# Row buffers opened ahead of retrieval, gathers paced to 31/32 of the dense steps, one inverse root on VectorE, the look-up in two pieces

## The chip, the cores and the metric

The kernel runs on one core of a Trainium2 chip. The metric is the device time of one execution in microseconds (us). TensorE, VectorE, ScalarE, POOL (GpSimd) and SyncE (which issues most of the DMAs) each work through their own instructions in order and wait for one another by semaphores. TensorE's clock has two levels, 1.2 and 2.4 GHz; the profile gives the granted clock as a share of the higher one.

## What is computed

One decoder block on 1024 tokens of width 1024, in float32: a gated DeltaNet and a sliding-window attention side by side, then an expert layer, a gated embedding, and a last norm. The change touches the expert layer and what follows it:

```
x = x + concat(o_dn, o_sw) @ w_out
h = rmsnorm(x, ffn_norm)
q = (h @ wq) per head and half;  sc = q @ keys          # 8 heads, 2 halves, 128 keys
top 16 of each half -> 256 sums -> top 16 of these       # expert = i1 * 128 + i2, gates = softmax
x = x + sum over 8 x 16 experts: gate * gelu(h . u[e]) * v[e]     # 16384 experts of width 1024
x = x + sigmoid(rmsnorm(x, ple_norm) @ w_gate) * (p @ w_proj)
out = rmsnorm(x, final_norm)
```

## The kernel before, in words

Tokens are worked on in 8 blocks of 128. `upstream` (L327) does the projections (`project`), the mixers (`mixing`: `deltanet` and `swa`) and, in four groups of two blocks, `retrieve` (L398): output projection, norm, queries, scores, top 16 of each half (`first_topk`), then `topk` (L757). Matmul operands are split into a high and a low float32r part, and three products are added up (`mm3`, L141).

The expert layer is done in two ways at once. Blocks 0 to 4 (`DBLK`) are dense: `topk` turns their choices into one-hot tiles, `gbuild` (L837) builds a table `gd` of gates for every expert and token, and `dense` (L924) goes over all 16384 experts in 128 tiles. Four tiles make a group (`cg`, 32 groups): for each tile `uT` and `v` are loaded and split, 48 matmuls form `bk_u`, ScalarE takes the gelu, VectorE multiplies by `Gt` and splits the result into `wh` and `wl`; then for 5 blocks and 2 halves 12 matmuls each form `bk_y`, which VectorE adds to `xB`. The banks of the first two blocks are held over all groups.

Blocks 5 to 7 (`ABLK`) are gathered: for each of 128 choices `fetched` (L856) has POOL issue an indirect DMA of one row for each of 128 tokens, from `u` and later from `v`. VectorE takes a dot product with `h2n` for each `u` row (L868) and adds each `v` row to `acc` with the weight from `dots` (L882). `h2n` and `acc` share one buffer. The 768 gathers are one generator (`gather_job`), and `dense` calls `step` (L946) 448 times, after each expert tile and each `bk_y`; a call advances the gathers to their share of the steps done. `held_back` puts each gathered row's VectorE work behind the dense work of `LAG` steps earlier.

Row buffers come in turns from two pools: even rows from `gp` (`GBUF`), odd ones from `gx` (`GXBUF`). `gp` also holds `h2n`/`acc` and `dots`. Both are opened after `upstream` (L1069, L1070), on the right side of SBUF, which is filled from its end: the pools of `retrieving` (L383; `lt` with `tv`, `tiu`, `sc`, `cand`, `get3` first, then `wp2`, `hp`, `sm2`, `bg`) have lain there before, and then come `xB` and the `v` tiles. A tile laid over an older one waits for that one's last reader.

The look-up in `topk` (L784 to L808) finds the two indices behind each of the 16 best sums by comparisons against starts, with tiles of 16 x KC x 8; KC = 16 is all in one piece.

`final` (L1013) takes the blocks in the order 5, 6, 0, 1, 2, 3, 4, 7: `pre` (L1033) loads a block, takes its norm (`norm`, L187: ScalarE's square sum, `rsqrt`, one VectorE step `h`) and transposes it; `post` (L1047) multiplies by the gate weights. These are loaded in 8 slices through two `raw` buffers and split into `wgh` and `wgl` (`gate_weights`, L1020). `rsqrt` (L154) is two POOL instructions: scale and add, then the power -0.5.

The order of instructions on each engine and in each DMA queue is not written by hand: a planner lays it out at build time from the program's order, the waits, and its own estimate of times. At run time each engine keeps to it.

Of the kernel before, what the change touches and what calls it, by code (L numbers as in the profile page):

```python
# [7 lines left out]
F32 = mybir.dt.float32  # L8
F32R = mybir.dt.float32r
BF = mybir.dt.bfloat16  # L10
I32 = mybir.dt.int32
U32 = mybir.dt.uint32
AF = mybir.ActivationFunctionType
ALU = mybir.AluOpType
# [4 lines left out]
P = 128  # L19
# [5 lines left out]
EPS = 1e-6  # L25
# [8 lines left out]
NU = len(DBLK) * 128  # L34
GC = 4
TB = 16
GBUF = 4
GXBUF = 3
RATE = 0.6
LAG = 2  # L40
HELD = 2
# [26 lines left out]
def block_kernel(ctx: ExitStack, tc, I, out, dbg=None):  # L68
# [9 lines left out]
    def tt(o, a, b, op):  # L78
        return V.tensor_tensor(o, a, b, op)  # L79

    def stt(o, a, s, b, op0, op1, **k):
        return V.scalar_tensor_tensor(o, a, s, b, op0, op1, **k)  # L82
# [65 lines left out]
    h2Td = [dr.tile([P, DK, NU], F32, name=f"h2Td{i}") for i in range(2)]  # L148
    gd = dr.tile([NE // GC, P, NT // TB, GC, TB], F32, name="gd")

    eidx = cp.tile([P, len(UBLK), P], I32, name="eidx")
    gate_a = cp.tile([P, len(UBLK), P], F32, name="gate_a")

    def rsqrt(pool, dst, src, scale, n):  # L154
        v = pool.tile([P, n], F32, tag=f"rsv{n}", name="rs_v", bufs=2)
        G.tensor_scalar(v, src, scale, EPS, op0=ALU.mult, op1=ALU.add)  # L156
        G.tensor_tensor(dst, v, mhalf[:, 0:n], ALU.pow)  # L157
# [169 lines left out]
    def upstream():  # L327
        with early as em:
            dn = em.enter_context(tc.tile_pool(name="dn", bufs=1, reuse_waits="tile"))
            psum(em, dn=2, de=1, sw=1)  # L330
            with ExitStack() as es:
                c1 = es.enter_context(tc.tile_pool(name="c1", bufs=1, side="right"))
                wp = es.enter_context(tc.tile_pool(name="wp", bufs=3, side="right"))
                sm = es.enter_context(tc.tile_pool(name="sm", bufs=2, side="right"))
                psum(es, acc=2, tp=2)
                projected(wp, sm)
                load_consts()
                mixw = row(c1, "mix_norm", D)
                convw = c1.tile([P, 12, 4], F32, name="convw")
                nc.sync.dma_start(convw, I["convw"])  # L340
                onorm = row(c1, "out_norm", P)
                V.tensor_scalar(onorm, onorm, 0.5, None, op0=ALU.mult)
                dtb = row(c1, "dt_bias", 4)
                nea = row(c1, "a_log", 4)
                S.activation(nea, nea, AF.Exp)
                V.tensor_scalar(nea, nea, -1.0, None, op0=ALU.mult)
                prevs = c1.tile([P, 12, 3], F32, name="prevs")
                halo[:] = [(mixw, convw, onorm, dtb, nea), prevs]
                rope_tables(sm, cos, sin)
                project(0, (c1, wp, sm))  # L350
                mixers = mixing(dn)
                mixers(0)
                project(1, (c1, wp, sm))
            with ExitStack() as es:
                lt = es.enter_context(tc.tile_pool(name="lt", bufs=1, side="right", reuse_waits="tile"))
                retrieve, half_built = retrieving(lt, es)
                for gi in range(len(GROUPS)):
                    if gi + 1 < len(GROUPS):
                        mixers(gi + 1)
                    elif HBLK:  # L360
                        half_built()
                    retrieve(gi)
# [394 lines left out]
    def topk(tk, bg, b, v, iu):  # L757
# [25 lines left out]
        tt(dx[:, 1:16], ix[:, 0, 1:16], ix[:, 0, 0:15], ALU.subtract)  # L783
        flat = cand.rearrange("p h c -> p (h c)")  # L784
        i1, i2 = flat[:, 0:P], flat[:, P:2 * P]
        KC = 16

        def summed(dst, x):
            for s in (1, 2, 4):
# [134 lines left out]
    def dense(xB):  # L924
        with ExitStack() as es:
# [20 lines left out]
            def step(ins):  # L946
                anchors.append(ins.ins)
                count[0] += 1
                n = total * count[0] // steps - count[1]
                count[1] += n  # L950
                advance(n)

# [60 lines left out]
    def final(xB):  # L1013
        with ExitStack() as es:
            fq = es.enter_context(tc.tile_pool(name="fq", bufs=1, reuse_waits="tile"))
            fp = es.enter_context(tc.tile_pool(name="fp", bufs=2, reuse_waits="tile"))
            cf = es.enter_context(tc.tile_pool(name="fc", bufs=1, reuse_waits="tile"))
            psum(es, g=4, tp=4)

            def gate_weights():  # L1020
                for k in range(DK):
                    hi = cf.tile([P, D], F32R, name=f"wgh{k}")
                    lo = cf.tile([P, D], F32R, name=f"wgl{k}")
                    raw = cf.tile([P, D], F32, tag="raw", name="raw", bufs=2)
                    nc.sync.dma_start(raw, I["wg"][k])
                    split(raw, hi, lo)
                    wg.append((hi, lo))

            wg = []
            plew = row(fp, "ple_norm", D, 1)  # L1030
            order = ABLK[:-1] + BBLK + ABLK[-1:]

            def pre(b):  # L1033
                if b in ABLK:
                    xt = fp.tile([P, D], F32, tag="xt", name="xt", bufs=3)
                    nc.sync.dma_start(xt, x1d[b])
                else:
                    xt = xB[:, b - BBLK[0]]
                pr = fq.tile([P, D], F32, tag="pr", name="pr", bufs=3)
                nc.sync.dma_start(pr, prd[b])  # L1040
                h = norm(fp, "h", xt, plew, 2)
                hh = fp.tile([P, DK, P], F32R, tag="hh", name="hh")
                hl = fp.tile([P, DK, P], F32R, tag="hl", name="hl")
                transpose_split("tp", h, hh, hl, slice(0, P))
                return b, xt, pr, hh, hl

            def post(b, xt, pr, hh, hl):  # L1047
                for j in range(2):
                    cs = slice(j * 512, (j + 1) * 512)
                    pg = bank("g")  # L1050
                    for dk in range(DK):
                        mm3(pg, hh[:, dk], hl[:, dk], wg[dk][0][:, cs], wg[dk][1][:, cs],
                            dk == 0, dk == DK - 1)
                    gt = fq.tile([P, 512], F32, tag="gt", name="gt", bufs=2)
                    S.activation(gt, pg, AF.Tanh, scale=0.5)
                    stt(gt, gt, 1.0, pr[:, cs], ALU.add, ALU.mult)
                    tt(xt[:, cs], gt, xt[:, cs], ALU.add)
                o = norm(fq, "o", xt, finw, 2)
                nc.sync.dma_start(out[b * P:(b + 1) * P, :], o)

            nxt = pre(order[0])
            gate_weights()
            finw = row(fq, "final_norm", D, 1)
            for i in range(NBLK):
                cur, nxt = nxt, pre(order[i + 1]) if i + 1 < NBLK else None
                post(*cur)

    upstream()
    pools["gp"] = ctx.enter_context(tc.tile_pool(name="gp", bufs=GBUF, side="right", reuse_waits="tile"))  # L1069
    pools["gx"] = ctx.enter_context(tc.tile_pool(name="gx", bufs=GXBUF, side="right", reuse_waits="tile"))  # L1070
    with tc.tile_pool(name="xB", bufs=1, side="right", reuse_waits="tile") as xp:
        xB = xp.tile([P, NB, D], F32, name="xB")
# [61 lines left out]
```

## Time and profile before

| | us |
|---|---|
| median of 3 runs | 3034.56 |
| lowest, highest | 3032.35, 3036.15 |
| the profiled execution | 3043.6 |
| its span, first to last instruction | 3041.8 |
| mean granted clock of TensorE | 0.986 |

The profile is one execution. Its page gives the busy time of each engine; views of the trace behind it show single instructions with their start, their length and, in brackets, how long the engine had been idle and what ended that idle time. PE is TensorE's matmuls, PEld its weight loads, DVE VectorE, ACT ScalarE, SP SyncE (SPq: the DMAs that it issues). L12 is line 12 of the kernel. Matmuls are pipelined, so their lengths overlap. Windows are counted from the start of the span.

### The profile page before, as it was taken

The page shows a single profiled execution, that of the slowest core. Times are in us where ns is not written, and L with a number is a line of the kernel's source. Part 1 is how long each engine was busy: PE and PEld are TensorE (multiplying, and loading weights), DVE is VectorE, ACT ScalarE, POOL GpSimd, SP SyncE. Part 2 cuts the span into 40 slices and gives each one's busy share as a digit, 9 for nine tenths or more (in the row PEclk, how much of TensorE's full clock was granted, in tenths as well). Part 3 has the DMA queues.
Part 4 walks back from the last instruction along what each step waited for, and adds up shares of the span by engine and source line. Part 5 has one row for each costly group of instructions (what it writes and reads, how often), then busy time and mean ns, then how long its engine had stood idle before and what let it go on. Part 6 is the DMA issues. An engine that isn't in the chain of part 4 may idle for free. (4 is left out here: it accounts for less than half of the span.)

```text
span 3041.8 us, 49726 instructions
## 1 busy us (share of the span) xinstructions
PE 2936.2 (97%) x18287; PEld 2690.0 (88%) x18287; DVE 2499.4 (82%) x5023; ACT 1234.6 (41%) x2761; POOL 1068.4 (35%) x901
## 2 busy tenths in 40 slices
PE   7999999999999889999999999999999999999988
PEld 5887999999998789999999989998898898998967
DVE  5658636898999779988699889887998898899974
ACT  5556634488777663222222222232232232222223
POOL 0000000000000000765356556554656565556541
PEclk9989999999999999999999999999999999999989
DMA  7569657689889994999799989888999899899962
GB/s 236 142 223 364 206 191 248 215 223 243 237 242 270 287 279 141 351 338 348 272 342 354 330 319 369 329 332 300 335 351 345 318 358 332 306 337 347 324 256 89
DMA packets 449955, 869.30 MB, mean 286 GB/s; under 512 B 193456, under 2 KB 235824, under 8 KB 445360
## 3 DMA queue, kind: packets, MB, share of 16 engines
q1 hardware_dynamic: 339120, 463.43, 46.5%
q0 software_dynamic: 110592, 402.70, 36.4%
q8 instruction: 143, 2.34, 0.3%
q14 instruction: 100, 0.82, 0.1%
HBM read 766.40 MB, written 99.61 MB: 285 GB/s over the span
## 5 line engine op out<-in xcount | busy, mean ns | idle before, releaser
L136 PE MATMUL bk_u<-hT,uh 128*128 128x320 f32 x4096 | 915.4, 310 | 7.0 <-DMA hT<-h2Td 3.7
L136 PEld LDWEIGHTS bk_u<-hT,uh 128*128 128x128 f32 x4096 | 695.7, 189 | 23.2 <-ACT ge L988 4.6
L858 POOL DMA_INDIRECT rows<-in_u_dram,eidx x384 | 499.1, 1300 | 555.5 <-DVE dots L868 283.1
L136 PE MATMUL bk_u<-hT,ul 128*128 128x320 f32 x2048 | 635.0, 310 | 0.3 <-DVE ul L79 0.3
L858 POOL DMA_INDIRECT rows<-in_v_dram,eidx x384 | 498.6, 1298 | 350.1 <-DVE acc L82 287.5
L82 DVE SCALAR_TENSOR_TENSOR acc<-rows,dots,acc 128x1024 f32<-128x1024 f32 x384 | 492.2, 1282 | 35.4 <-DMA rows<-in_v_dram,eidx 24.5
L868 DVE CUSTOM_DVE_ANT_0 rows<-rows,h2n 128x1024 f32<-128x1024 f32 x384 | 459.9, 1223 | 27.5 <-DMA rows<-in_u_dram,eidx 27.3
L136 PEld LDWEIGHTS bk_u<-hT,ul 128*128 128x128 f32 x2048 | 386.5, 189 | 4.1 <-DVE ul L79 0.7
L988 ACT ACTIVATE ge<-bk_u 128x320 f32<-128x320 f32 x256 | 109.8, 431 | 603.3 <-PE bk_u L136 552.6
L136 PE MATMUL bk_y<-vh,wh 128*128 128x512 f32 x768 | 298.9, 391 | 3.0 <-DVE xB L79 3.0
L136 PE MATMUL bk_y<-vl,wh 128*128 128x512 f32 x768 | 299.9, 392 | 0.0
L136 PE MATMUL bk_y<-vh,wl 128*128 128x512 f32 x768 | 296.8, 393 | 2.6 <-DVE wl L79 2.6
L76 ACT ACTIVATE wh<-ge 128x320 fp32r<-128x320 f32 x256 | 118.7, 469 | 316.7 <-DVE ge L79 304.1
L76 ACT ACTIVATE o<-o,tT 128x128 f32<-128x128 f32 x640 | 204.5, 392 | 56.4 <-DVE o L79 55.1
L76 ACT ACTIVATE uh<-ur 128x1024 fp32r<-128x1024 f32 x128 | 135.3, 1057 | 226.4 <-PE bk_u L136 217.5
L136 PE MATMUL bk_gm<-o 128*128 128x128 f32 x1280 | 203.2, 286 | 22.5 <-ACT o L76 16.2
L136 PE MATMUL bk_s<-h,whi 128*128 128x256 f32 x1024 | 209.1, 295 | 3.3 <-DMA whi<-wqc 1.0
L79 DVE TENSOR_TENSOR o<-iota,tT 128x1024 f32<-128x1024 f32 x160 | 194.7, 1220 | 11.5 <-PE bk_gm L136 8.9
L136 PEld LDWEIGHTS bk_gm<-o 128*128 128x128 f32 x1280 | 178.2, 195 | 29.0 <-ACT o L76 20.2
L136 PE MATMUL bk_yp<-vl,wh 128*128 128x512 f32 x512 | 199.7, 391 | 0.0
L136 PE MATMUL bk_yp<-vh,wh 128*128 128x512 f32 x512 | 199.1, 391 | 0.0
L79 DVE TENSOR_TENSOR xB<-bk_y,xB 128x512 f32<-128x512 f32 x192 | 131.1, 689 | 79.5 <-PE bk_y L136 79.1
(302 smaller groups left out, 5840.5 us busy)
## 6 DMA issues: line engine op xcount, KB each, us to landing
ur<-in_uT_dram SPq DMA_DIRECT2D x128, 512.0 KB, 6.8
vr<-in_v_dram SPq DMA_DIRECT2D x128, 512.0 KB, 6.7
gd<-stage SPq DMA_DIRECT2D x40, 1024.0 KB, 7.3
Gt<-gd SPq DMA_DIRECT2D x32, 1280.0 KB, 9.6
wlo<-wqc SPq DMA_DIRECT2D x128, 256.0 KB, 4.6
whi<-wqc SPq DMA_DIRECT2D x128, 256.0 KB, 4.7
whi<-woc SPq DMA_DIRECT2D x64, 256.0 KB, 4.8
wlo<-woc SPq DMA_DIRECT2D x64, 256.0 KB, 4.7
```

The source lines that it names most:

```text
L76: return S.activation(o, i, AF.Copy, **k)
L79: return V.tensor_tensor(o, a, b, op)
L82: return V.scalar_tensor_tensor(o, a, s, b, op0, op1, **k)
L136: PE.matmul(o, l, r, start=start, stop=stop)
L858: G.indirect_dma_start(out=r, out_offset=None, in_=tab, in_offset=bass.IndirectOffsetOnAxis(ap=eidx[:, u, s:s + 1], axis=0))
L868: held_back(V.tensor_tensor_reduce(out=r, in0=r, in1=h2n, op0=ALU.mult, op1=ALU.add, scale=1.0, scalar=0.0, accum_out=dots[:, s:s + 1]))
L988: S.activation(ge, pa, AF.Gelu_apprx_tanh)
```

## The change

`gp` is opened within `upstream`, ahead of the retrieval pools, with three row buffers instead of four; `gx`, still opened afterwards, gets four instead of three. The look-up runs twice on halves. `step` divides by 31/32 of the steps. The first `pre` of `final` uses an inverse root on VectorE: an integer first guess from the bits, then three Newton rounds, twelve instructions on 128 x 1.

```diff
@@ -34,8 +34,8 @@
 NU = len(DBLK) * 128
 GC = 4
 TB = 16
-GBUF = 4
-GXBUF = 3
+GBUF = 3
+GXBUF = 4
 RATE = 0.6
 LAG = 2
 HELD = 2
@@ -148,10 +148,23 @@
     h2Td = [dr.tile([P, DK, NU], F32, name=f"h2Td{i}") for i in range(2)]
     gd = dr.tile([NE // GC, P, NT // TB, GC, TB], F32, name="gd")
 
+    newton = [False]
     eidx = cp.tile([P, len(UBLK), P], I32, name="eidx")
     gate_a = cp.tile([P, len(UBLK), P], F32, name="gate_a")
 
     def rsqrt(pool, dst, src, scale, n):
+        if newton[0]:
+            v, i, t = (pool.tile([P, n], d, tag=f"rn{m}{n}", name="rn_" + m)
+                       for m, d in (("v", F32), ("i", I32), ("t", F32)))
+            V.tensor_scalar(v, src, scale, EPS, op0=ALU.mult, op1=ALU.add)
+            V.tensor_scalar(i, v.bitcast(I32), 1, None, op0=ALU.logical_shift_right)
+            V.tensor_scalar(i, i, -1.0, 1597463007.0, op0=ALU.mult, op1=ALU.add)
+            y = i.bitcast(F32)
+            for it in range(3):
+                tt(t, y, y, ALU.mult)
+                stt(t, t, -0.5, v, ALU.mult, ALU.mult)
+                stt(dst if it == 2 else y, t, 1.5, y, ALU.add, ALU.mult)
+            return
         v = pool.tile([P, n], F32, tag=f"rsv{n}", name="rs_v", bufs=2)
         G.tensor_scalar(v, src, scale, EPS, op0=ALU.mult, op1=ALU.add)
         G.tensor_tensor(dst, v, mhalf[:, 0:n], ALU.pow)
@@ -351,6 +364,7 @@
                 mixers = mixing(dn)
                 mixers(0)
                 project(1, (c1, wp, sm))
+            pools["gp"] = ctx.enter_context(tc.tile_pool(name="gp", bufs=GBUF, side="right", reuse_waits="tile"))
             with ExitStack() as es:
                 lt = es.enter_context(tc.tile_pool(name="lt", bufs=1, side="right", reuse_waits="tile"))
                 retrieve, half_built = retrieving(lt, es)
@@ -783,7 +797,7 @@
         tt(dx[:, 1:16], ix[:, 0, 1:16], ix[:, 0, 0:15], ALU.subtract)
         flat = cand.rearrange("p h c -> p (h c)")
         i1, i2 = flat[:, 0:P], flat[:, P:2 * P]
-        KC = 16
+        KC = 8
 
         def summed(dst, x):
             for s in (1, 2, 4):
@@ -946,7 +960,7 @@
             def step(ins):
                 anchors.append(ins.ins)
                 count[0] += 1
-                n = total * count[0] // steps - count[1]
+                n = min(total, total * count[0] // (steps * 31 // 32)) - count[1]
                 count[1] += n
                 advance(n)
 
@@ -1058,7 +1072,9 @@
                 o = norm(fq, "o", xt, finw, 2)
                 nc.sync.dma_start(out[b * P:(b + 1) * P, :], o)
 
+            newton[0] = True
             nxt = pre(order[0])
+            newton[0] = False
             gate_weights()
             finw = row(fq, "final_norm", D, 1)
             for i in range(NBLK):
@@ -1066,7 +1082,6 @@
                 post(*cur)
 
     upstream()
-    pools["gp"] = ctx.enter_context(tc.tile_pool(name="gp", bufs=GBUF, side="right", reuse_waits="tile"))
     pools["gx"] = ctx.enter_context(tc.tile_pool(name="gx", bufs=GXBUF, side="right", reuse_waits="tile"))
     with tc.tile_pool(name="xB", bufs=1, side="right", reuse_waits="tile") as xp:
         xB = xp.tile([P, NB, D], F32, name="xB")
```

## Rows read from the trace of the kernel before

**Rows 1.** Page, part 1: busy time of TensorE, its share of the span, instructions.
```profile
PE 2936.2 (97%) x18287; PEld 2690.0 (88%) x18287; DVE 2499.4 (82%) x5023; ACT 1234.6 (41%) x2761; POOL 1068.4 (35%) x901
```

**Rows 2.** Windows: length, busy time (x instructions) of each engine, PEclk, DMA share, GB/s.
```profile
900.00:1125.00 225.00, 198.45 (x1523) 191.96 (x1522) 195.63 (x652) 157.15 (x433) 4.74 (x6) 0.95 0.97 272
...
1171.00:2907.00 1736.00, 1726.38 (x9649) 1569.76 (x9648) 1526.20 (x2190) 459.06 (x747) 979.34 (x755) 1.00 0.90 327
2920.00:2940.00 20.00, 6.17 (x19) 4.29 (x18) 16.87 (x17) 6.37 (x9) 8.33 (x10) 0.60 0.72 266
2940.00:3033.00 93.00, 92.42 (x433) 76.44 (x431) 52.51 (x64) 34.79 (x59) 13.19 (x24) 0.99 0.28 102
...
1125.00:1227.00 102.00, 100.14 (x567) 91.78 (x566) 89.47 (x329) 35.79 (x56) 9.73 (x8) 0.98 0.55 192
```

**Rows 3.** Timeline of TensorE at the join: start, length, instruction [idle before <-releaser].
```profile
2932.81 1.97 PE L139 MATMUL bk_tp<-ident,h 128*128 128x128 f32 x8 [12.44 <-DVE h L82]
```

**Rows 4.** Timeline of ScalarE at the join.
```profile
2913.00 1.06 ACT L190 ACTIVATE h<-xt 128x1024 f32<-128x1024 f32 x1 [16.69 <-DMA xt<-x1d]
```

**Rows 5.** Timeline of POOL at the join.
```profile
2924.88 1.86 POOL L858 DMA_INDIRECT rows<-in_v_dram,eidx  x1 [0.78 <-DVE acc L82]
2926.81 0.19 POOL L156 TENSOR_SCALAR rs_v<-ss 128x1 f32<-128x1 f32 x1
```

**Rows 6.** Timeline of VectorE at the join.
```profile
2928.95 2.60 DVE L82 SCALAR_TENSOR_TENSOR acc<-rows,dots,acc 128x1024 f32<-128x1024 f32 x2 [3.02 <-DMA rows<-in_v_dram,eidx]
2931.48 1.28 DVE L82 SCALAR_TENSOR_TENSOR h<-xt,rs,ple_norm 128x1024 f32<-128x1024 f32 x1
```

**Rows 7.** Timeline of SyncE's queue at the join: first loads of gate weights.
```profile
2918.81 0.81 SPq L1025 DMA_DIRECT2D raw<-in_wg_dram  x2
```

**Rows 8.** Tile raw of the gate weights: durations min/median/max ns, first and last start.
```profile
L76 ACT ACTIVATE wgh<-raw x8: 1056/1060/1066, 2926.2 to 2956.7; 128x1024 fp32r<-128x1024 f32 x8
L79 DVE TENSOR_TENSOR wgl<-raw,wgh x8: 1220/1224/1226, 2932.7 to 2957.8; 128x1024 fp32r<-128x1024 f32 x8
...
DMA to landing us min/median/max: 3.4/4.9/9.4
```

**Rows 9.** Timeline of POOL, 1129 to 1221 us: the first gathers.
```profile
1129.55 1.21 POOL L858 DMA_INDIRECT rows<-in_u_dram,eidx  x1 [106.17 <-PE bk_s L136]
...
1220.28 0.94 POOL L858 DMA_INDIRECT rows<-in_u_dram,eidx  x1 [47.07 <-DVE cand L79]
```

**Rows 10.** Windows of 56 us in dense, columns as in Rows 2.
```profile
1787.00:1843.00 56.00, 51.74 (x277) 46.71 (x276) 45.21 (x73) 13.67 (x21) 35.99 (x25) 0.94 0.88 317
...
2851.00:2907.00 56.00, 56.00 (x316) 50.97 (x315) 50.04 (x58) 12.25 (x21) 32.45 (x26) 1.00 0.89 314
```

**Rows 11.** Groups by line and shape, VectorE: a small instruction, busy us, mean ns.
```profile
L816 DVE RECIPROCAL gs<-gs 128x8 f32<-128x8 f32 x8 | 1.7, 206 | 0.0
```

**Rows 12.** Timeline of VectorE, 1066 to 1070 us: two pieces of the look-up and what follows.
```profile
1066.16 1.22 DVE L79 TENSOR_TENSOR get<-get,tix 128x2048 bf16<-128x2048 bf16 x1
1067.29 0.09 DVE L753 MATCH_VALUE_LOAD tkr<-tv,sc 128x8 f32 x1
...
1068.69 0.69 DVE L79 TENSOR_TENSOR get<-get 128x1024 bf16<-128x1024 bf16 x1
1069.29 0.29 DVE L754 MAX8 tv<-tkr 128x8 f32<-128x128 f32 x1
```

**Rows 13.** Who waited for whom, TensorE, 900 to 1125 us: total, times, longest.
```profile
PE bk_gm L136 <- ACT o L76: 14.2, 15, 2.7
```

**Rows 14.** Who waited for whom, SyncE's queue, 1760 to 1850 us.
```profile
SPq L884 <- DVE acc L82: 14.5, 1, 14.5
```

**Rows 15.** Timeline of SyncE's queue, the load of xB.
```profile
1129.40 0.37 SPq L937 DMA_DIRECT2D xB<-x1d  x1
```

**Rows 16.** Timeline of VectorE, 1153 to 1172 us.
```profile
1153.75 0.27 DVE L79 TENSOR_TENSOR cand<-tv 128x128 f32<-128x128 f32 x1
...
1171.64 0.69 DVE L79 TENSOR_TENSOR xB<-bk_y,xB 128x512 f32<-128x512 f32 x1
```
## The prediction

> **What bounds the kernel now.** I read the page first. TensorE is busy 2936.2 of 3041.8 us [rows 1], so only two things can shorten the run: TensorE's idle time, and time that it spends at the lower clock. Then I cut the run into stretches by a table of windows [rows 2]. Reading them, look at the first number after the length (TensorE's busy time) and at the granted clock. Retrieval between 900 and 1125 us has 198.45 busy of 225 at 0.95. The dense stage has 1726.38 of 1736 at 1.00: nothing is to be won in it, and it sets the pace for all else. The join from dense to final, 2920 to 2940 us, has 6.17 busy of 20 at a mean clock of 0.60 (so mostly at 1.2 GHz, the lower of the two levels; TensorE sat idle in it). The final stage after it has 92.42 of 93. So the join is the one place where some 14 us lie open, and I followed it engine by engine.
>
> TensorE ends dense at 2920.37 and waits 12.44 us for `h`, the first normalised block [rows 3]. ScalarE gets that block at 2913.00, having waited 16.69 us for its load [rows 4] while the DMA engines carried row gathers. Its sum of squares is there at 2914.1, but POOL, in order, still issues gathers until 2926.74 and only then forms the inverse root [rows 5]. VectorE, in order too, waits 3.02 us for gathered rows, adds two of them, and reaches `h` at 2931.48 [rows 6]. Gathers stand before the final stage on three queues. Behind this lies a second chain: the eight gate-weight slices go through two raw buffers, are first loaded at 2918.81 (two loads, [rows 7]), and the last low part starts at 2957.8 [rows 8].
>
> The gathers themselves start late. Four are issued from 1129.55 on, and the flow begins at 1220.28 [rows 9], because row buffers lie on retrieval's tiles. 768 gathers at 448 steps make a plan of 1.71 a step.
>
> **The end: pacing and the inverse root.** 448*31//32 is 434, and 14 steps make one group of four expert tiles, so the plan of gathers ends one group before dense does. A group is 312 matmuls, and a window of 56 us holds 316 [rows 10]: some 55 us. From 1220.28 to 2924.88 there are some 764 gathers, 2.23 us each. Their order on VectorE is fixed by the planner, and the new plan, 1.77 a step, is 25 gathers a group or 2.2 us each. So the old rate holds the new plan, but hardly catches up a late start. How late it is decides whether gathers end near 2880 or near 2920; I come to that below. In either case the inverse root no longer stands behind POOL's gathers: twelve small VectorE instructions take its place. No row shows them; the nearest is a reciprocal of 0.206 us [rows 11], so 12 of these give 2.5 us, and half that if they overlap as other VectorE work does. POOL does it in two steps, the first of 0.19 us [rows 5]; even were these free, the move costs 2.5 us at most, in a group in which TensorE is occupied till 2920. I take it as nothing: the cover is the last dense group, and without it up to 2.5 us would be paid.
>
> What is late next is the weights. Their first loads wait for dense's last matmuls, and the change does not touch that: 2918.81 stays. From there to the end of the last low part, 2957.8 + 1.2 = 2959.0, the four pairs took 40.2 us. With gathers gone a pair needs a landing of 4.9 us (median), 1.06 on ScalarE, 1.22 on VectorE [rows 8] and about 0.5 for the hand-overs (an estimate: the last high part ends at 2956.7 + 1.06, the last low part starts within 0.1 us of that, and the next load's issue has no row), so 7.7: four make 31 us, and the last part is ready at 2949.7, **9.3 us earlier**. Bounds: landing 3.4 gives 25 us, 15 earlier; 9.4 for the first pair, gathers still flowing, gives 5 earlier. TensorE's rest after the last weight, 3033 - 2959 = 74 us, is unchanged, as it is full there [rows 2]; starting some 10 us earlier it finishes up to 3 us more before that weight. I take **-10 us**, between -5 and -16.
>
> **The look-up in two pieces.** KC = 8 runs the loop body of 18 VectorE instructions twice on halves. Start to start a piece of 2048 takes 1.13 us and one of 1024 takes 0.60 [rows 12], so each extra instruction costs 0.07 by starts, and 0.69 x 2 - 1.22 = 0.16 by durations: 1.3 to 2.9 us for each block. I take 1.3, since neighbours overlap. Blocks 0 to 5 come before dense: 7.8 us of VectorE. It is busy 195.63 of 225 us in the last retrieval stretch [rows 2], where TensorE waits 14.2 us for the scaled one-hot tiles `o` [rows 13] that stand behind VectorE. The look-ups of blocks 4 and 5 fall there and I charge them whole, 2.6 us; for the earlier four TensorE is mostly the later one. **+2.5 us**, between 0 and 7.8.
>
> The Trainium skill, Perfetto Trace Analysis, section Optimizing Scalar/DVE Operations, has a rule that would turn this sign: an engine that is not saturated but causes bubbles elsewhere may finish sooner when its instructions are broken up. By it this term would be a gain; VectorE at 87% does not show which side of "saturated" it is on. It is a rival below.
>
> **Row buffers opened ahead.** Three row buffers, the block's `h2n` and `dots` get room of their own (16.5 KB), so the first gathers and dot products no longer wait for retrieval's tiles. The four buffers of gx come to lie on lt instead, whose last look-up tiles are read until the flow begins at 1220. So even rows can flow early and odd ones not. VectorE is busy 89.47 of the 102 us from 1125 to 1227 [rows 2]: 12.5 us are room for ten dots of 1.22 us (as long as a low part of a weight, [rows 8]). Ten gathers at 2.23 bring the gathers' end from 2925 to about 2900. Nothing on TensorE moves by this alone: **0**, between -2 and +5 from crowding on VectorE.
>
> **Sum**: -10 + 2.5 + 0 = -7.5, say -8 with the little that is done before the last weight. The profiled execution took 3043.6 us (span 3041.8), 9.0 above the median of the runs, 3034.56. It gives 3035.6 on its own scale; taken off the median, **3026.6 us**.
>
> **Rivals.**
> (a) *A new stall in dense takes it back.* SyncE's queue is in order. At the first block switch the store of `acc` waited 14.5 us for VectorE [rows 14] with dense's loads behind it, and the stretch has 277 matmuls instead of 316 [rows 10]: 39 of 0.177 us, 6.9 us. Today the third such store comes after dense's loads; paced, it comes among those of the last group. Against: the second switch cost little. Then -8 + 7 = -1: 3033.6. Chance 0.12.
> (b) *The change doesn't reach the end.* If gathers still run until 2920 and VectorE's order keeps `h` behind them, only the landing of the first pair matters: -5 + 2.5, less what crowding costs, about -2: 3032.5. Chance 0.08.
> (c) *More than forecast.* The switch at 1790 is a matter of a static order; with another order its 6.9 us may go. Or the finer look-up lets `o` in sooner: 15 waits shortened by at most 1.13 - 0.60 = 0.53 us each are 8 us, which is what the rule above would give here. Then -15: 3019.6. For it: the 14.2 us. Against: the extra work on a nearly full engine. Chance 0.11, the rule's part 0.04.
> (d) *Slower: the load of `xB`.* The right side of SBUF is filled from its end: first gp, then lt, by its tiles now 16,608 bytes a partition, with `tv` outermost. After retrieval gx takes 16,384 of these, and `xB`, next, lies on the 224 left, in the first `tv`; before, it lay wholly on other pools. Its load, issued at 1129.40 [rows 15], must now wait for block 6's candidates, the last of which is read at 1153.75; `xB` is first needed at 1171.64 [rows 16]. The load is 2.6 MB, 9.6 us at the 272 GB/s before it [rows 2]. Spare time is about 8 us. If block 6's candidates slip past 1162, as early dots could make them, TensorE stands, and in SyncE's queue the next expert loads stand behind. To be slower than before by over 6 us it has to slip to 1176. Price of a slip to 1182: 20 us, so -8 + 20 = +12: 3046.6. Chance 0.13.
>
> **Numbers.** 0.2% (6 us here) is about what a measurement of this kernel can tell from no change. The forecast has 0.56; its own range is -13 to -3 (the bounds of the three terms are not all met at once), and some three quarters of it is past -6: 0.43, with 0.13 within. With (c) faster is 0.54; with (a) and (b) the same is 0.33; slower is (d), 0.13. The range goes from the deeper end of (c), 3013, to the upper side of (a), 3040, and leaves out (d) and a little at the low end.
>
> **What would show it.** Right: the gap before the first transpose of the final stage falls from 12.44 us to under 5; the first norm's inverse root is on VectorE and ends before 2920; the last gather is issued before 2915 on this scale, the last group has few or none; the last `wgl` starts some 9 us sooner after the first `raw` load; retrieval's windows lengthen by 2 to 3 us. Wrong: matmul counts of a dense stretch that fall under 305 where they did not before (a, d), `xB` issued late with TensorE idle behind it (d), a last `wgl` that is still 40 us behind the first load (b), or retrieval longer by over 6 us.

## The result and the profile after

The changed kernel takes 3062.78 us (median of 4 runs, 3061.96 to 3063.75), the kernel before beside it 3035.36 us (4 runs, 3032.35 to 3037.89): a ratio of 1.0091, 95% interval 1.0073 to 1.0108. It is **slower by some 27 us**, where 8 us less were forecast and the range ended at 3040. The profiled execution after has a span of 3059.9 us. One execution of run 7 below and one of the kernel before beside runs 9 and 10 took over 4000 us; the ratios leave them out.

The first question is where TensorE loses time. The windows of the kernel before, for three stretches that [rows 2] did not cut this way (columns as there):

```profile
1125.00:1200.00 75.00, 73.14 (x420) 67.44 (x419) 65.33 (x285) 26.55 (x43) 4.02 (x4) 0.98 0.55 189
1200.00:1300.00 100.00, 100.00 (x564) 91.24 (x563) 90.24 (x157) 27.35 (x44) 58.74 (x42) 1.00 0.85 313
1300.00:2900.00 1600.00, 1590.38 (x8892) 1446.31 (x8891) 1400.89 (x1916) 423.22 (x690) 915.70 (x709) 1.00 0.91 332
```

The same windows of the kernel after, with the last stretch of retrieval ahead of them:

```profile
900.00:1125.00 225.00, 191.22 (x1460) 183.26 (x1458) 198.11 (x687) 157.91 (x436) 9.99 (x11) 0.95 0.94 274
1125.00:1200.00 75.00, 64.99 (x372) 60.75 (x372) 70.84 (x307) 23.84 (x37) 9.48 (x8) 0.91 0.56 185
1200.00:1300.00 100.00, 81.53 (x419) 70.74 (x418) 89.63 (x160) 24.67 (x39) 60.14 (x44) 0.91 0.84 307
1300.00:2900.00 1600.00, 1595.31 (x8908) 1449.84 (x8907) 1406.80 (x1906) 419.72 (x683) 921.10 (x711) 1.00 0.91 335
```

From 1125 to 1300 us TensorE does 791 matmuls where it did 984: 193 fewer. 24 of them belong to retrieval, which the kernel after has finished before 1125 us; the other 169 are dense's own (`bk_u`, `bk_y`, `bk_yp`: 791 against 960), and at the pace of the long stretch after it (1600 us for 8892) they are some 30 us. From 1300 on the two keep step. So the loss is at the start of dense. SyncE's DMA queue there, after; compare [rows 15], where the load of `xB` is issued at 1129.40, directly behind the first `Gt`:

```profile
1129.10 0.33 SPq L983 DMA_DIRECT2D Gt<-gd  x1
1138.08 0.34 SPq L971 DMA_DIRECT2D ur<-in_uT_dram  x1
...
1186.22 0.33 SPq L971 DMA_DIRECT2D ur<-in_uT_dram  x1
1194.87 0.33 SPq L976 DMA_DIRECT2D vr<-in_v_dram  x1
1195.24 0.43 SPq L951 DMA_DIRECT2D xB<-x1d  x1
1233.19 0.33 SPq L971 DMA_DIRECT2D ur<-in_uT_dram  x1
```

Between `Gt` and `xB` now stand eleven other loads. VectorE over the same time (the timeline; compare [rows 16], first `xB` add at 1171.64):

```profile
1131.42 0.27 DVE L79 TENSOR_TENSOR cand<-tv 128x128 f32<-128x128 f32 x1
...
1183.93 1.12 DVE L79 TENSOR_TENSOR cand<-tv 128x128 f32<-128x128 f32 x9
...
1211.32 0.29 DVE L82 SCALAR_TENSOR_TENSOR eidx<-cand 128x128 int32<-128x128 f32 x1
1211.53 1.28 DVE L79 TENSOR_TENSOR xB<-bk_y,xB 128x512 f32<-128x512 f32 x2
```

The first add has no wait in brackets: it simply stands behind the whole of the last look-up, which ends with `eidx`, 39.9 us later than in [rows 16]. The waits of TensorE from 1120 to 1300 us (total, times, longest) and, under them, the longest one on ScalarE in the timeline:

```profile
PE bk_y L136 <- DVE xB L79: 13.7, 4, 11.9
PE bk_u L136 <- ACT ge L1002: 9.4, 3, 7.9
PE bk_yp L136 <- ACT wh L76: 4.1, 1, 4.1
PE bk_yp L136 <- DVE wl L79: 3.3, 2, 2.7
```

```profile
1224.55 0.83 ACT L76 ACTIVATE wh<-ge 128x320 fp32r<-128x320 f32 x2 [29.98 <-PE bk_y L136]
```

TensorE cannot use its `bk_y` banks again without the adds, ScalarE cannot fill `wh` without TensorE, and SyncE's next `ur` load (1233.19) waits in turn: one late add stops the whole ring.

The join between dense and final did get shorter. VectorE there, and TensorE's first transposes (compare [rows 6] and the 12.44 us of [rows 3]):

```profile
2945.52 0.69 DVE L79 TENSOR_TENSOR xB<-bk_y,xB 128x512 f32<-128x512 f32 x1 [2.06 <-PE bk_y L136]
2946.13 0.14 DVE L159 TENSOR_SCALAR rn_v<-ss 128x1 f32<-128x1 f32 x1
...
2951.53 0.16 DVE L82 SCALAR_TENSOR_TENSOR rs<-rn_t,rn_i 128x1 f32<-128x1 f32 x1
2951.73 1.28 DVE L82 SCALAR_TENSOR_TENSOR h<-xt,rs,ple_norm 128x1024 f32<-128x1024 f32 x1
```

```profile
2953.07 4.00 PE L139 MATMUL bk_tp<-ident,h 128*128 128x128 f32 x16 [7.58 <-DVE h L82]
```

The weights and the end, as groups by tile (least, median and longest ns, first and last start):

```profile
L79 DVE TENSOR_TENSOR wgl<-raw,wgh x8: 1215/1223/1225, 2948.6 to 2970.1; 128x1024 fp32r<-128x1024 f32 x8
L136 PE MATMUL bk_g<-wgh,hh x128: 388/394/772, 2956.7 to 3049.7; 128*128 128x512 f32 x128
L872 POOL DMA_INDIRECT rows<-in_v_dram,eidx x384: 932/1014/2483, 1442.2 to 2898.8; - x192
```

The last gather is issued at 2898.8, 26 us earlier than in [rows 5] and 47 us ahead of the last `xB` add at 2945.5. I measure the join from the last `xB` add to the last gate matmul: before it is 2921.4 to 3031.6, 110.2 us; after 2945.5 to 3049.7, 104.2 us. So 6.0 us are won at the end. The last `xB` add comes 24.1 us later, which leaves 18.1 us, the difference of the two spans. The medians differ by 27.4 us, since the profiled execution of the kernel before is 8 us above its median, and where those 8 us lie no row shows.

### The profile page after: what moved, and what is told of

Same layout as the page of the kernel before. It is cut to its first block, busy times and chain, and to the rows that moved or that the text cites. A ratio compares the mean times of both kernels' runs of the same rounds, so it can differ in the third digit from the quotient of the medians.

```text
span 3059.9 us, 49900 instructions
## 1 busy us (share of the span) xinstructions
PE 2936.3 (96%) x18287; PEld 2687.2 (88%) x18287; DVE 2515.0 (82%) x5179; ACT 1232.6 (40%) x2761; POOL 1065.6 (35%) x899
## 5 line engine op out<-in xcount | busy, mean ns | idle before, releaser
L136 PE MATMUL bk_u<-hT,uh 128*128 128x320 f32 x4096 | 916.1, 311 | 15.8 <-ACT ge L1002 11.5
L872 POOL DMA_INDIRECT rows<-in_u_dram,eidx x384 | 507.5, 1322 | 532.9 <-DVE dots L882 313.2
L872 POOL DMA_INDIRECT rows<-in_v_dram,eidx x384 | 490.4, 1277 | 365.6 <-DVE acc L82 291.5
L76 ACT ACTIVATE vh<-vr 128x1024 fp32r<-128x1024 f32 x128 | 131.8, 1053 | 168.8 <-PE bk_y L136 124.6
```

Of the source, the lines that this page charges most:

```text
L76: return S.activation(o, i, AF.Copy, **k)
L136: PE.matmul(o, l, r, start=start, stop=stop)
L872: G.indirect_dma_start(out=r, out_offset=None, in_=tab, in_offset=bass.IndirectOffsetOnAxis(ap=eidx[:, u, s:s + 1], axis=0))
```

## The experiments

Twelve kernels were run, each timed over five rounds beside the kernel before, whose medians in the four groups of runs were 3036.46, 3036.78, 3036.65 and 3036.22 us.

**1. `xB` moved off `tv`** (the kernel after, with 256 bytes a partition between `gx` and `xB`):

```diff
     pools["gx"] = ...
+    gap = ctx.enter_context(tc.tile_pool(name="gap", bufs=1, side="right", reuse_waits="tile"))
+    gap.tile([P, 64], F32, name="gap")
     with tc.tile_pool(name="xB", ...
```

> The changed kernel with 256 bytes a partition left free between gx and xB, so that xB no longer lies on tv; all else is kept. Theory 1 (the 224 bytes on tv make the planner put the load of xB late in SyncE's queue, and TensorE pays): the load is issued before 1150 us, no idle time of TensorE over 5 us before 1260 us ends on xB, and the time falls by some 30 us from 3062.8 to 3025 to 3036. Theory 2 (early dot products crowd VectorE between 1100 and 1260 us and delay all behind them): the load is early but TensorE still loses 20 us or more there, and the time stays over 3048. Theory 3 (the half-size look-up makes retrieval and the start of dense longer): likewise over 3048.

Measured: 3040.78 us (12 runs), ratio to before 1.0015 (1.0004 to 1.0025): 22.0 us less than after. The load is early, as the first theory has it, and no wait of TensorE ends on `xB`; the time lies between the expected ranges, 5 us above the first. Its load of `xB`, and its windows:

```profile
1125.33 4.31 SPq L951 DMA_DIRECT2D xB<-x1d  x1
```

```profile
1125.00:1200.00 75.00, 57.49 (x301) 51.76 (x300) 70.25 (x313) 22.48 (x35) 12.47 (x11) 0.86 0.62 213
1200.00:1300.00 100.00, 98.93 (x559) 90.02 (x559) 88.43 (x165) 30.15 (x48) 47.25 (x39) 1.00 0.83 288
1300.00:2900.00 1600.00, 1598.97 (x8977) 1457.07 (x8976) 1414.30 (x1922) 426.42 (x694) 926.49 (x716) 1.00 0.92 336
```

256 bytes put the load back to 1125 us and give back the stretch from 1200 to 1300. The stretch before it stays poor (301 matmuls against 420), and dense after 1300 is fuller than before (8977 against 8892). Two things besides `xB` are at work, and they nearly cancel.

**2. Early opening and the look-up's halves alone** (the kernel before with `gp` opened ahead, three and four row buffers, KC = 8; old pacing, old inverse root):

```diff
+            pools["gp"] = ctx.enter_context(tc.tile_pool(name="gp", bufs=GBUF, ...))  # in upstream
-GBUF = 4
-GXBUF = 3
+GBUF = 3
+GXBUF = 4
-        KC = 16
+        KC = 8
```

> The kernel before with gp opened ahead (3 and 4 buffers) and KC = 8, without the new pacing and without the inverse root on VectorE. Theory 1: the load of xB is late as in the changed kernel, so the start of dense costs the same 30 us, and the end gains little: 3060 to 3075. Theory 4 (the loss comes from the tighter pacing): within 6 us of before, 3029 to 3041.

Measured: 3058.56 us (6 runs), ratio 1.0075 (1.0057 to 1.0093). The load of `xB` is at 1193.7 here too, and the time is 1.4 us under the first range: the loss needs neither the pacing nor the new inverse root.

**3. Pacing and inverse root alone** (the kernel before with the two edits of the end):

```diff
-                n = total * count[0] // steps - count[1]
+                n = min(total, total * count[0] // (steps * 31 // 32)) - count[1]
+            newton[0] = True
             nxt = pre(order[0])
+            newton[0] = False
```

> The kernel before with the pacing of 31/32 and the inverse root on VectorE alone. Theory 1: the load of xB stays early, the join of dense and final gets shorter by 5 to 10 us, 3025 to 3031. Theory 4: slower than before by 15 us or more. If gathers that start late cannot keep the tighter plan, the join does not change: 3032 to 3038.

Measured: 3046.91 us (10 runs), ratio 1.0035 (1.0023 to 1.0047). None of the three ranges holds. The end got worse by itself: 115.0 us from the last `xB` add (2920.4) to the last gate matmul (3035.4), and the last gather at 2923.8, where [rows 5] has 2924.88.

**4. The look-up's halves alone** (the kernel before):

```diff
-        KC = 16
+        KC = 8
```

> The kernel before with KC = 8 alone. By the term of the prediction +2.5 us (0 to 7.8): 3035 to 3043. Theory 3: slower by 15 us or more, over 3050. If finer pieces let the one-hot tiles in sooner: under 3031.

Measured: 3048.85 us (6 runs), ratio 1.0048 (1.0032 to 1.0064), 12 us slower by the medians, between the first two ranges. Its window at the start of dense, TensorE's longest wait there, and two rows of VectorE, the first product with `Gt` and the first instruction of a half look-up:

```profile
1125.00:1200.00 75.00, 57.42 (x306) 51.45 (x306) 70.97 (x317) 26.78 (x38) 3.33 (x4) 0.86 0.49 175
```

```profile
PE bk_yp L136 <- ACT wh L76: 17.6, 1, 17.6
```

```profile
1141.75 0.49 DVE L79 TENSOR_TENSOR ge<-ge,Gt 128x320 f32<-128x320 f32 x1
...
1150.61 0.67 DVE L79 TENSOR_TENSOR get<-pos,sel_b 128x1024 bf16<-128x1024 bf16 x1
```

Between 500 and 900 us this kernel does 3318 matmuls against 3252, so retrieval goes faster with the halves. But as dense begins the planner's order has other work on VectorE ahead of what dense's first `wh` needs: from 1125.0 to 1141.7 us the top 16 of the last scores, the choice among one block's sums, and three splits of `v`. (In the kernel before, VectorE takes the product with `Gt` at 1132.9, ahead of these.) ScalarE waits 13.6 us for `ge` from VectorE ahead of that `wh`, and TensorE stands 17.6 us, until 1142.8. The half look-ups themselves begin only at 1150.61, so it is the new order, and not the work of the halves, that stands in the way.

**5 and 6. Pacing and inverse root, each by itself** (the kernel before; run 5 with the `newton[0]` lines of run 3's diff, run 6 with its `n = min(...)` line).

> The kernel before with one edit: the inverse root of the final layer norm as 12 VectorE instructions in place of ScalarE's square root and VectorE's reciprocal. Theory: this edit is what made the run with pacing and inverse root 10 us slower than before, because its instructions stand on VectorE's in-order queue among the adds to acc and the gathers' weights, so that h comes late: about 3045 us, with the last xB add to the last bk_g at about 115 us, against 110.2 before. Rival: the pacing of the gathers did it, by what it moves on the queues during the dense steps; then this run is at 3033 to 3037 us, and the transposes start no later after the last xB add than before.

> The kernel before with one edit: the plan of the gathers reaches its end at 31/32 of the dense steps. Theory (the inverse root did the harm): 3033 to 3038 us; the last gather stays within 3 us of 2924.9, because the late first gather and not the plan sets it. Rival (the pacing did it): about 3045 us, with the loss inside the dense steps (last xB add later than 2926) or in the join.

Measured: the inverse root alone 3043.22 us (12 runs), ratio 1.0024 (1.0012 to 1.0036); the pacing alone 3040.82 us (12 runs), ratio 1.0021 (1.0011 to 1.0030). By medians 6 and 4 us, together the 10 of run 3 (by the ratios some 7 and 6, so that they add up only roughly): neither theory alone. The old inverse root is two POOL instructions (`rsqrt`), not ScalarE's square root and a reciprocal, as the expectations of runs 5 and 7 say. VectorE and TensorE in the run with the inverse root:

```profile
2926.24 0.15 DVE L159 TENSOR_SCALAR rn_v<-ss 128x1 f32<-128x1 f32 x1
...
2927.48 1.23 DVE L79 TENSOR_TENSOR wgl<-raw,wgh 128x1024 fp32r<-128x1024 f32 x1
...
2928.70 1.27 DVE L82 SCALAR_TENSOR_TENSOR acc<-rows,dots,acc 128x1024 f32<-128x1024 f32 x1
...
2933.68 0.15 DVE L82 SCALAR_TENSOR_TENSOR rs<-rn_t,rn_i 128x1 f32<-128x1 f32 x1
```

```profile
2936.28 3.67 PE L139 MATMUL bk_tp<-ident,h 128*128 128x128 f32 x16 [20.24 <-DVE h L82]
```

Twelve instructions of 0.15 us last 7.6 us, since others of 1.2 us stand between them. The pacing alone leaves the last gather at 2919.3, 3.5 us behind the last `xB` add (2915.8), as before (2924.9 and 2921.4). What its 4 us are was not found; its profiled execution is one of the short ones (span 3036.9).

**7. Gap, and the old inverse root** (run 1 without the new inverse root):

```diff
-            newton[0] = True
+            newton[0] = False
             nxt = pre(order[0])
```

> The kernel after, with 256 bytes put between gx and xB (so that xB lies off tv) and the inverse root back on ScalarE and VectorE's reciprocal; 3040.8 us with the gap alone. Theory: behind the gap, with the gathers done 25 us before the dense end, VectorE's queue is short there and the inverse root's place hardly matters, so 3038 to 3042 us, join of 102 to 106 us. Rival: the inverse root costs its 10 us here too, 3031 us, join under 98 us.

Measured: 3038.26 us (12 runs), ratio 1.0012 (1.0003 to 1.0022). Time and join are where the theory put them. Against run 1 it is 2.5 us by medians, but the two intervals nearly coincide, so that a cost of the new inverse root behind the gap is not clear of noise. The transposes come 1.98 us after dense ends, 5.6 us sooner than with the new root, but the join still takes 102.0 us against 103.9: TensorE then waits 3.57 us for the operand instead, and its first gate matmuls run at a granted clock of 0.50.

**8. Gap, old inverse root, KC = 16** (run 7 with the old look-up, and the gap widened to 4464 bytes since `lt` is longer then):

```diff
-        KC = 8
+        KC = 16
-    gap.tile([P, 64], F32, name="gap")
+    gap.tile([P, 1116], F32, name="gap")
```

> As the run with gap and the old inverse root, but with the look-up's old chunk of 16 (KC = 16), and the gap widened to 4464 bytes since the old tile is longer: what is left of the change is the early opening, the row buffers' numbers and the pacing. Theory: KC = 8 costs 12 us here as it did alone, through the exp of gate_a that stands in front of wh on ScalarE's queue as the dense steps begin: 3027 to 3031 us, faster than both kernels, with about 420 matmuls from 1125 to 1200 us against 301. Rival: with gathers already running at the start of the dense steps the start is slow whatever the look-up's chunk: 3037 to 3042 us and some 300 to 340 matmuls in that stretch.

Measured: 3053.94 us (6 runs), ratio 1.0058 (1.0044 to 1.0073). **Both expectations missed.** The start of dense is full again (413 matmuls from 1125 to 1200), as the theory had it, and yet the kernel is 16 us slower than with the halves:

```profile
1125.00:1200.00 75.00, 72.47 (x413) 67.06 (x414) 62.67 (x217) 27.37 (x42) 13.92 (x13) 0.95 0.71 233
1200.00:1300.00 100.00, 100.00 (x547) 89.45 (x546) 91.64 (x224) 26.66 (x43) 38.60 (x32) 1.00 0.74 257
1300.00:2900.00 1600.00, 1592.15 (x8843) 1436.98 (x8842) 1395.36 (x1901) 421.61 (x687) 914.33 (x707) 1.00 0.91 332
```

It loses 134 matmuls against run 1 in the long stretch (125 against run 7), 57 of them in the two stretches of 100 us that hold stalls near 1825 and 2395 us, where TensorE sinks to 7.2 of 10 us at a mean clock of 0.83; the rest is strewn. And from 500 to 1125 us it does 53 fewer than run 7 (4729 against 4782), some 7 us. So the costs of KC = 8 and of the early opening do not add up: each static order has its own stalls, and KC = 8 is a loss of 12 us in one and a gain of 16 us in the other.

**9. `xB` on `lt`, `tv` with it, in the kernel before** (`xB`'s pool opened ahead of `gp` and `gx`):

```diff
+    xp = ctx.enter_context(tc.tile_pool(name="xB", bufs=1, side="right", reuse_waits="tile"))
+    xB = xp.tile([P, NB, D], F32, name="xB")
     pools["gp"] = ...
     pools["gx"] = ...
-    with tc.tile_pool(name="xB", bufs=1, side="right", reuse_waits="tile") as xp:
...
```

> The kernel before with one edit: xB's pool is opened ahead of gp and gx, so that xB (20,480 bytes a partition) lies on lt and with it on tv, and the row buffers lie inward of it. Nothing of the change is in it. Theory (xB on tv is the cause by itself): the load of xB falls behind the last block's candidates, near 1195 us, the first xB add behind the last look-up, near 1205 us, TensorE stands for some 15 us between 1190 and 1220, SyncE's and ScalarE's queues with it, and the time is 3052 to 3062 us. Rival (the overlap costs only beside KC = 8 and gathers that already flow): load late, but less than 8 us lost, 3036 to 3044 us.

Measured: 3055.41 us (6 runs), ratio 1.0070 (1.0054 to 1.0086): 18.8 us slower, by this edit alone. The load, the first add, TensorE's wait and its windows:

```profile
1203.34 0.38 SPq L937 DMA_DIRECT2D xB<-x1d  x1
```

```profile
1203.02 0.29 DVE L82 SCALAR_TENSOR_TENSOR eidx<-cand 128x128 int32<-128x128 f32 x1
1212.69 1.29 DVE L79 TENSOR_TENSOR xB<-bk_y,xB 128x512 f32<-128x512 f32 x2 [9.38 <-DMA xB<-x1d]
```

```profile
1213.43 0.79 PE L136 MATMUL bk_y<-vh,wh 128*128 128x512 f32 x1 [25.21 <-DVE xB L79]
```

```profile
1190.00:1200.00 10.00, 0.00 (x0) 0.00 (x0) 9.62 (x20) 0.31 (x1) 0.00 (x0) 0.54 0.00 0
1200.00:1210.00 10.00, 0.00 (x0) 0.00 (x0) 3.14 (x6) 0.00 (x0) 0.00 (x0) 0.50 0.53 189
1210.00:1220.00 10.00, 6.57 (x19) 5.26 (x20) 7.26 (x13) 0.00 (x0) 3.87 (x3) 0.60 0.49 176
```

The load stands behind eleven other loads, as in the kernel after. But here `xB` lies on nearly all of `lt` (20,480 of 20,832 bytes), so that it also waits at run time, 19.4 us, for the very last look-up (issued 0.32 us after `eidx` starts), and everything else stands: no DMA for ten microseconds, no matmul for twenty. The row buffers lie elsewhere too. So this run shows that an overlap of `xB` with `lt` costs about as much without the rest of the change, but it does not price the 224 bytes by themselves; runs 1 and 10 do.

**10. Gap, old inverse root, old pacing** (run 7 with the old plan, which is run 2 with the gap):

```diff
-                n = min(total, total * count[0] // (steps * 31 // 32)) - count[1]
+                n = min(total, total * count[0] // steps) - count[1]
```

> The kernel after with the 256 bytes between gx and xB, the old inverse root and the old pacing: what is left of the change is the early opening, the buffers' numbers and KC = 8. Beside the run of the early opening and KC = 8 alone (3058.6 us) it has only the gap more. Theory: the gap gives back its 22 us here too, 3034 to 3038 us, with the load of xB near 1123 us. If pacing's cost as found alone (6 us) carries over, it ends 2 to 4 us under the run with gap and old root, 3038.3 us. Rival: the gap helped only beside pacing and the new root; then over 3045 us.

Measured: 3042.74 us (11 runs), ratio 1.0024 (1.0015 to 1.0033). The gap gives 15.8 us back here instead of 22, and the load is at 1126.9. The second part missed: without pacing it is 4.5 us slower than run 7, not faster (the two intervals just overlap), so pacing, which cost 4 us alone, does not cost them here. The last gather is at 2928.7 (run 7: 2894.4), yet the join is 102.3 us (run 7: 102.0).

**11 and 12. Gathers held back at the start of dense** (runs 7 and 8, with the plan begun after 28 steps):

```diff
-                n = min(total, total * count[0] // (steps * 31 // 32)) - count[1]
+                n = min(total, total * max(0, count[0] - 28) // (steps * 31 // 32 - 28)) - count[1]
```

> The run with gap and old inverse root (3038.3 us), with the gathers' plan begun only after 28 dense steps (about where that run stood at 1200 us) and still ended at 31/32. There 13 dot products of 1.22 us each stood on VectorE between 1116 and 1200 us, where the kernel before has none and TensorE waited for VectorE's and ScalarE's parts of the dense steps. Theory (early dots crowd the start of dense): no dots before 1200, TensorE idle 1120 to 1150 down from 17 us to under 8, 3026 to 3032 us, faster than both kernels. Rival (KC = 8 by its order slows the start, as alone): 300 to 320 matmuls from 1125 to 1200 as before the edit, 3036 to 3042 us.

> The same with KC = 16 and the wider gap of 4464 bytes (3053.9 us without the delay). Both suspects for the slow start of dense are out: no early dots, and the look-up as before. Theory: 410 to 430 matmuls from 1125 to 1200 us, 54 or more gelus done by 1300 us as in the kernel before (56; 50 without the delay), last gather still 15 us or more ahead of the last xB add, 3028 to 3036 us. Rival (the loss of that run lies in stalls at the switches of gathered blocks, not at the start): 3044 us or more.

Measured: 3067.35 us (4 runs), ratio 1.0093 (1.0076 to 1.0110), and 3066.79 us (4 runs), ratio 1.0097 (1.0080 to 1.0114). On the time both missed by far (the rival's "3044 us or more" holds for run 12 as a number only), for a reason that neither named. On the start of dense they answer: with KC = 8 it stays slow without a single early dot (314 matmuls from 1125 to 1200), so there it is the order that comes with the halves. The early dots cost nothing that shows at this place: 313 matmuls with them and 314 without at KC = 8 (runs 7 and 11), 413 and 407 at KC = 16 (runs 8 and 12). With KC = 16 the delayed kernel stays close to the kernel before up to the end of dense:

```profile
1125.00:1200.00 75.00, 73.74 (x407) 67.60 (x408) 72.66 (x288) 28.63 (x44) 0.96 (x1) 0.96 0.42 149
1300.00:2900.00 1600.00, 1592.57 (x8864) 1438.31 (x8863) 1399.27 (x1925) 421.58 (x688) 912.00 (x708) 1.00 0.91 333
```

```profile
L79 DVE TENSOR_TENSOR xB<-bk_y,xB x192: 662/686/695, 1168.6 to 2927.6; 128x512 f32<-128x512 f32 x192
L872 POOL DMA_INDIRECT rows<-in_v_dram,eidx x384: 932/1015/2516, 1507.7 to 2964.8; - x192
L136 PE MATMUL bk_g<-wgh,hh x128: 387/389/794, 2942.7 to 3050.2; 128*128 128x512 f32 x128
```

The last gather now comes 37 us *after* dense, on top of the weights, and the join takes 122.6 us (run 12; 120.4 in run 11). The plan asked for 1.89 gathers a step; the flow did not follow it. POOL's instructions from 1300 to 2900 us, nearly all of them gathers, are 709 before, 711 after, 716 in run 1 and 708 in run 12, under plans from 1.71 to 1.89 a step.

## Why the prediction was wrong

**The load of `xB`, rival (d): the step that failed.** The sum gives the overlap of `xB` with `tv` nothing, on the ground that 8 us are to spare; it costs 22.0 us (run 1 against after) and 15.8 (run 10 against run 2), and a wider overlap in the kernel before costs 18.8 (run 9). Rival (d) had the place and the 224 bytes right, and its sign came: `xB` issued late with TensorE idle behind it. Its condition failed, and with it the chance of 0.13: "If block 6's candidates slip past 1162, as early dots could make them, TensorE stands". They did not slip. The first of the last two blocks reads `tv` at 1131.42, even earlier than before, and the second at 1183.93; the load left only at 1195.24, right behind a `vr` load, and the add behind the last `eidx` had no wait at all. I took the overlap for a wait at run time with 8 us to spare, measured against the old order. It acted at build time: the planner, told of one more dependence, laid out the load eleven places later in SyncE's queue and the first adds behind a whole look-up. That the price of 20 us comes near is partly luck: it was worked out for a load at 1182 and an add that waits for it, while the first add came 39.9 us later than before. That the tile in question is the last block's, not the one last read at 1153.75, fits the load's place between 1186 and 1195; no row shows which of the two `tv` tiles lies there.

**The join, -10.** Measured -6.0. The weights did as forecast and a little more. The last low part is ready 25.8 us after the last `xB` add (2970.1 + 1.2 - 2945.5) against 37.6 before, 11.8 earlier. From the first `raw` load to the last low part it is 27.4 us (2943.9 to 2971.3), where 31 were forecast and 40.2 stood before. What failed is "TensorE's rest after the last weight, 3033 - 2959 = 74 us, is unchanged": it went from 72.6 to 78.4 us, since less had been done before it. From the first transpose to the last gate matmul it takes 98.8 us before and 96.6 after: nearly all of it is work of TensorE's own, so what counts is how soon it may begin. That wait fell from 12.44 to 7.58 us, not under 5.

**The inverse root, nothing, 2.5 us at most.** The instructions are even shorter than estimated (0.15 us), but an in-order queue is paid in places, not durations. Alone it cost 6 us (run 5), strewn over 7.6 us among gathers and weights; in the changed kernel it started behind the last `xB` add, though its sum of squares had been ready since 2933.9, so that the last dense group was no cover, and took 5.6 us. What that is worth behind the gap, 2.5 us by medians (run 7 against run 1), is not clear of noise.

**Pacing.** That "the old rate holds the new plan, but hardly catches up a late start" held: alone it moved the last gather's distance to the last `xB` add by nothing. The earlier end comes from an earlier start and the tighter plan together: the last gather is 26.9 us ahead of the last `xB` add in run 7, 6.4 us in run 10, which differs from it by the old plan, and 3.5 us behind it before. But the join gains as much in run 10 as in run 7, so the last 20 us of it buy nothing there.

**KC = 8, +2.5, and row buffers, 0.** Both were costed by VectorE's time, and neither by what the new order does to dense's first steps. KC = 8 alone cost 12 us, nearly all as waits at the start of dense. The Trainium skill's rule that breaking up instructions may let work be done sooner (Perfetto Trace Analysis, Optimizing Scalar/DVE Operations) agrees with run 4 between 500 and 900 us, where TensorE does 66 matmuls more; its gain did not reach the end by itself. From 500 to 1125 us together it is 38 more (4813 against 4775, some 5 us), and in the kernel after 5 more, so that retrieval got neither 2 to 3 us longer nor 8 us shorter there. The early opening put 13 dots of 1.22 us on VectorE between 1116 and 1200 us in runs 7 and 8 (9 in the kernel after), where none had stood; runs 11 and 12 show no cost of them at that place.

**The other rivals.** (b) did not come: the gathers did end early. (a)'s stall did not come at the last switch; the one at the first is still there, 2.2 us idle at 1790 us and a clock of 0.83 in the ten us after. (c)'s hope that this stall goes came true in runs 1, 2 and 7, where no window of ten us from 1300 to 2900 us has a clock under 1.00. That is not a matter of the early opening or of KC = 8 alone: run 10 has both and shows 0.83 at 1310 and at 2400 us, and run 9 has neither and shows no such window.

**The sum as it came out**, from before to after by medians (+27.4): the overlap +22.0 (run 1), the rest +5.4. In run 1's trace that rest is 124 matmuls fewer from 1125 to 1300 us (860 against 984, 22 us), 85 more from 1300 to 2900 (15 us), and the join's -6.3: about +1 in these single executions, whose spans differ by 1.2 us the other way; the profiled execution of the kernel before is 8 us above its median and that of run 1 less than 2, which accounts for the rest. The two halves are as large as the overlap; that they nearly cancel is luck.

No run beat the kernel before; the nearest is run 7, slower by 0.12% (0.03% to 0.22%).

## What to carry to other kernels

Where a planner or a pool lays out order and memory, ask of each moved or resized tile not only when its old readers end but what the plan does with one more dependence: look for the big load that changes place in its queue, and for the instructions that now stand behind a stage that they do not need. A few hundred bytes of padding may decide it, so measure the layout apart from the idea. Gains of parts found one at a time need not add where each part draws a new static order; and a producer that lags behind its plan does not end earlier by a tighter plan alone: here it took an earlier start as well.

## What was not expected of the hardware

The flow of gathers kept nearly one rate under plans from 1.71 to 1.89 a step: 693 (run 2, early start and old plan) to 716 (run 1) gathers in the 1600 us from 1300 on in all fourteen kernels, 2.2 to 2.3 us each, with the DMA engines' mean share at 0.90 to 0.92. Among the kernels that open `gp` early and have KC = 8, the old plan gave the fewest (693 and 705 in runs 2 and 10, 711 to 716 in the others). POOL waits there mostly for VectorE to free a row buffer (in the kernel before 294 us on `dots` and 289 on `acc`), and a row needs 7 us (median) to land. Whether seven buffers, VectorE's order or the DMA engines set the rate was not tried.

TensorE's clock makes a stall dearer than its length: in run 9 the granted clock is 0.54 and 0.50 in the two windows in which TensorE stands, still 0.60 in the one in which it starts again, which holds 19 matmuls in 6.57 us of work, and 1.00 in the next.
